# Second token mixer of a two-layer decoder trunk: shared token differences, one-instruction blends, outputs summed by channel, and a new order of the work

## The chip, the cores and the metric

The kernel runs on one core of one Trainium2 chip. That core has a matrix engine (TensorE, PE in the profile, with its weight loads as PEld), a vector engine (VectorE, DVE), a scalar engine (ScalarE, ACT), GpSimd (POOL) and a sync engine (SP) that issues the transfers. The metric is the device time of one execution in microseconds; the median of three runs before the change is 1159.81 us.

## The reference, cut to what matters

The trunk has two layers over 256 tokens of width 1024. Each is a half-step SwiGLU block, a token mixer and another half-step SwiGLU block, all between RMS norms. Layer 0 mixes with sparse attention and a state-space branch, layer 1 with RWKV-7. The change is in the second mixer, and the order of both mixers is set anew:

```python
def rwkv7_time_mix(h, mu, w_r, w_k, w_v, w_o, w0, w1, w2, a0, a1, a2, g1, g2, k_k, k_a, r_k, ln_g, ln_b):
    xx = pad(h, one token)[:, :-1] - h                    # difference to the token before
    xr, xw, xk, xv, xa, xg = [h + xx * mu[i] for i in range(6)]
    r, k, v = xr @ w_r, xk @ w_k, xv @ w_v
    w = -softplus(-(w0 + tanh(xw @ w1) @ w2)) - 0.5
    a = sigmoid(a0 + (xa @ a1) @ a2)
    g = sigmoid(xg @ g1) @ g2
    ...
    def step(state, inp):                                 # 16 heads of 64 channels, 256 steps
        sa = einsum('bhij,bhj->bhi', state, -kk_t)
        state = state * d_t + sa[..., None] * (kk_t * a_t) + v_t[..., None] * k_t
        return state, einsum('bhij,bhj->bhi', state, r_t)
    ...
    y = (y - mean) * rsqrt(var + eps)                     # by head
    y = y * ln_g + ln_b + sum(r * k * r_k) * v
    return (y * g) @ w_o
```

## The kernel before, in words

Tokens lie in two tiles (t = 0, 1) of 128, channels in eight blocks of 128. The recurrence is worked in its chunked form: each token tile is a chunk, and each chunk has two halves of eight heads, so four quarters q = 2t + half.

The stages of the second mixer (function `mix1`) are written as generators, here called strands. The parts that matter:

- `mix_k` and `mixed` blend the normed input `hT` (channels by tokens) with the token before it. `share_past` and `share_now` give the two factors mu and 1 - mu. A blend takes two instructions: `present` makes h times (1 - mu) in a small tile `mixt` on ACT or DVE, and a second one on DVE adds mu times the shifted input. There are 16 blends of 128x128 for the keys and 24 of 128x256 for r, v and the gate.
- `project_k`, `project_r`, `project_v`, `gate_in` and `gate_out` are the projections. `project_v` and `work_o` (the output projection) use three matmuls per product, with high and low parts of both operands; such three are called a triple here.
- `products` and `stored` make the triangle matrices `LT` (matmul `acc<-kk,beT`). `invert32` inverts their 32x32 diagonal blocks on DVE in 31 serial steps (tiles `lb`, `tm`, `tt`, `lc`). `invert` joins the blocks, quarter by quarter, with small matmuls (`tm,LT`, `xw,lc`, `lc,xw`, `xw,LT`, `LT,xw`) and small copies on ACT and DVE between them.
- `grams` makes three 128x128 score matrices per head, with 64 of the array's rows each (`rhT,beT`, `kk,aT`, `rhT,aT`), and `masked` multiplies them by a mask on DVE into the tiles `G` (`Gx` for quarter 2).
- `evac_v` takes the values out of PSUM: eight ACT passes over 64 columns each, with a sum, into `vc`, then on DVE the bonus product `yB` and the subtraction of the mean.
- `head` forms u for a quarter, and the carried state `Z`. `outs` forms the outputs y of a quarter: eight matmuls with the scores as weights (128 columns) and the values as the moving side (64 columns), for chunk 1 four matmuls with `rhT` as weights and Z moving, and eight more scores times u, all into one PSUM tile with tokens on the partitions. Then come the square, the norm by head, the gate, and a transpose (`tp<-ident,xu`) for the output projection.

The order is set by a planner, `_Plan`. It keeps an estimated free time for each engine and each buffer; `run` repeatedly takes the strand whose next step has the lowest sum of earliest start and priority, and every instruction is emitted on its engine in that order, which the build keeps. The priorities are the tables `PRIORITY` (second mixer) and `PRIORITY0` (first mixer). PSUM has four buffers for sums (list `pa`, tile `acc`) and two for transposes (list `pt`, tile `tp`); SBUF has `SLOTS` = 21 slots of 1024 columns.

All engine calls go through the helper `_Engine`, so that the profile gives nearly every instruction line 141; instructions are told apart by their tiles.

Of the kernel before, what the change touches and what calls it, by code (L numbers as in the profile page):

```python
# [18 lines left out]
P = 128  # L19
# [141 lines left out]
class _Strand:  # L161
    def __init__(self, gen, prio, light):
        self.gen, self.prio, self.light, self.engine, self.begin, self.end = gen, prio, light, None, 0.0, 0.0
        self.step()
# [10 lines left out]
class _Plan:  # L175
# [3 lines left out]

    AFTER = {"pe": 200.0, "act": 45.0, "dve": 45.0, "sp": 2000.0}  # L180

    def __init__(self, **free):
        self.free = {"pe": 0.0, "act": 0.0, "dve": 0.0, "sp": 0.0, **free}
        self.events, self.strands, self.now, self.users, self.load = {}, [], None, {}, []
# [35 lines left out]
    def count(self, engine, name, out, a, k):  # L220
# [5 lines left out]
        if engine == "pe":  # L226
            if name == "transpose":
# [3 lines left out]
            else:  # L231
                m = 1
                for i in a[0].shape[1:]:
                    m *= i
# [34 lines left out]
    def run(self):  # L269
        while self.strands:  # L270
            ready = [(t + s.prio + (s.light * max(0.0, self.idle(t) - 0.4) if s.light else 0.0), i) for i, s in enumerate(self.strands) if (t := self.start(s)) is not None]
# [12 lines left out]
class _Trunk:  # L284
    PRIORITY = {"factors": 100, "evac_k": 0, "products": 200, "stored": -500, "evac_r": 93, "bonus": 352, "evac_v": 417,
                "masked": -500, "second": 206, "project_k": 250, "lora": -500, "decay": 74, "rates": 73, "keys": 149,
                "invert32": 500, "mixed": -265, "split_x": -455, "project_r": 300, "gate_in": 300, "split_v": 164,
                "project_v": 406, "gate_out": 800, "grams": 43, "invert": -500, "tokens": 416, "head": 581, "outs": 869,
                "split_o": 500, "work_o": 928, "finish": 709, "ahead": 1099, "mix_k": 80}
    PRIORITY0 = {"scale": 500, "normed": 282, "work_a": 300, "end_k": 249, "end_q": -300, "end_r": -389, "split_a": 0, "split":  # L290
                 100, "project": 300, "convolved": 204, "gate": 0, "compress": -366, "attend": 141, "scores":
                 200, "values": 100, "steps": 213, "products0": 410, "tokens0": 163, "carry": 647, "decays":
                 -17, "weights": 300, "outputs": 141, "gated": 195, "project_out": 497, "summed": 324,
                 "finish": 98, "split_f": 330, "second": 200}
# [1516 lines left out]
    def mix1(self, ph, gpost, y1):  # L1811
# [3 lines left out]
        H, N, SLOTS = 16, 64, 21  # L1815
# [46 lines left out]
        pa, pt, ml, xl, gml, gl, lwl, hl, ll, rl = [0.0] * 4, [0.0] * 2, [0.0] * 3, [], [0.0], [], [0.0], [], [], [0.0] * 4  # L1862
# [3 lines left out]
        for key, n, l in (("w2", 2, lwl), ("a2", 2, lwl), ("hT", 7, xl), ("xk", 1, xl), ("rows", 1, xl), ("lc", 4, sl),  # L1866
                          ("lws", 2, xl), ("XW0", 2, xl), ("XW1", 2, xl), ("rowb", 2, sl), ("rowg", 4, sl),
                          ("gtk", 2, sl), ("btk", 2, sl), ("tm", 4, hl), ("Z", 4, lwl)):
            share(key, n, l)
# [20 lines left out]
        xk = self.xp.tile([P, KD, S], F32, name="mix", tag="x8")  # L1890

# [53 lines left out]
        def mix_k(t):  # L1945

            for k in range(KD):
                e = plan.sooner("act", "dve")
                yield e, ml
                m = mt([P], "mixt")  # L1950
                present(e, m, 2, k, P * t, P * t + P)
                yield "dve"
                nc.vector.scalar_tensor_tensor(xk[:, k, TS[t]], *self.share_past(2, k, P * t, P * t + P), m, op0=ALU.mult, op1=ALU.add)
                give(ml)
                fire("xk", t, k)
            drop("hT")

        def second():
# [27 lines left out]
            add(mix_k(1), pr["mix_k"])  # L1986
# [271 lines left out]
        def mixed(name, i, buffers):  # L2258

            for k in range(KD):  # L2260
                e = plan.sooner("act", "dve")
                yield e, ml, ev("h"), *([buffers] if k == 0 else [])
                if k == 0:
                    X[name] = (self.xp if name == "r" else mp).tile([P, KD, S], F32, name="mix", tag="x8" if name == "r" else "mix")
                m = mt([S], "mixt")
                present(e, m, i, k, 0, S)
                yield "dve"
                nc.vector.scalar_tensor_tensor(X[name][:, k], *self.share_past(i, k, 0, S), m, op0=ALU.mult, op1=ALU.add)
                give(ml)
            drop("hT")  # L2270
# [91 lines left out]
        def evac_v(t, c, a):  # L2362
# [3 lines left out]
            yield "act", *([] if vc[t] else [sl])  # L2366
# [7 lines left out]
            nc.vector.tensor_scalar(mean, mean, -1.0 / N, None, op0=ALU.mult)  # L2374
# [3 lines left out]
            yield "dve"  # L2378
# [463 lines left out]
```

## Time and profile before

| | |
|---|---|
| median of the runs | 1159.81 us (1159.47 to 1159.92) |
| profiled execution | 1158.96 us, of which span 1157.2 us |
| PE busy | 1137.4 us, 98% |
| DVE busy | 941.3 us, 81% |
| ACT busy | 679.8 us, 59% |
| granted PE clock | 0.998 |
| second mixer | about 741 to 967 us of the span |

A row of the view by order of time has start, length, engine, line, operation, and tiles as out<-in; for a matmul the moving operand stands first and the weights second, then rows*columns of the array that it uses, then the size of the result, and the number of rows that were put together. An f32 matmul leaves two such rows, one in the rounded format (the triples and the bulk of the SwiGLU blocks) one. In the view of windows, a window's start and end are followed by its length and by the busy time and count of each engine. In the view of groups, a busy sum and the mean of one in ns are followed by the engine's idle time before the group and what ended it.

### The profile page before, as it was taken

Reading aid. Unit: us, or ns where it says so; the run is one execution under the profiler, and the core shown is the slowest. Engines: PE = TensorE matmul, PEld = TensorE weight load, DVE = VectorE, ACT = ScalarE, POOL = GpSimd, SP = SyncE. Lnnn points to the kernel's source line nnn. Section 1 sums busy time; section 2 is a strip of 40 time slices with the busy share of each in tenths; the row PEclk is TensorE's granted clock in tenths of the full one; section 3 lists DMA queues with packets and bytes.
Section 4 is the critical chain, followed back from the end, with each engine's and each line's share of the span. In section 5 each row is a group of like instructions: output and inputs, shape, how many; then the busy total and the mean of one; then the engine's idle time right before and its main releaser. Section 6 shows DMA issues by size and latency. Waiting matters only on the chain.

```text
span 1157.2 us, 17665 instructions
## 1 busy us (share of the span) xinstructions
PE 1137.4 (98%) x6771; PEld 959.0 (83%) x6771; DVE 941.3 (81%) x1495; ACT 679.8 (59%) x1105; POOL 17.2 (1%) x46
## 2 busy tenths in 40 slices
PE   9999999999999999999999999999999999999997
PEld 7788888888988778888888888799988797888885
DVE  6696697898779889977889969678885798899694
ACT  6655465677574786655687755475054135877461
POOL 0000000000000000000000000002100000000000
PEclk9999999999999999999999999999999999999999
DMA  8857535433334735735462845611333022718631
GB/s 281 288 190 242 193 128 186 149 129 109 110 125 161 268 121 204 251 146 197 160 262 95 296 173 217 229 38 50 120 111 146 20 109 92 309 55 278 228 118 68
DMA packets 50131, 192.42 MB, mean 166 GB/s; under 512 B 6205, under 2 KB 6205, under 8 KB 46334
## 3 DMA queue, kind: packets, MB, share of 16 engines
q1 hardware_dynamic: 50046, 191.29, 46.4%
q8 instruction: 53, 0.87, 0.3%
q14 instruction: 32, 0.26, 0.1%
HBM read 190.22 MB, written 1.05 MB: 165 GB/s over the span
## 4 chain that ended last, share of the span: by engine, by line
PE 76%; DVE 9%; DMA 6%; ACT 5%; issue 3%; SPq 0%; DVEq 0%; ACTq 0%
PE acc L141 72%; PE tp L141 4%; DVE wlo L141 3%; DMA raw<-in_wst_dram 3%; ACT whi L141 2%; DMA hx<-in_wst_dram 2%; DMA wa<-in_wst_dram 1%; ACT junk L141 1%; DVE hx L141 1%; DVE rs_a L141 1%; ACT hx L141 1%; ACT wa L141 0%; DVE suml L141 0%; DVE rs_y L141 0%; DVE x L141 0%
## 5 line engine op out<-in xcount | busy, mean ns | idle before, releaser
L141 ACT ACTIVATE whi<-raw,gch 128x1024 fp32r<-128x1024 f32 (+2 forms) x187 | 186.1, 1016 | 95.8 <-DMA raw<-in_wst_dram 76.3
L141 DVE SCALAR_TENSOR_TENSOR wlo<-raw,gch,whi 128x1024 fp32r<-128x1024 f32 (+2 forms) x187 | 204.4, 1113 | 38.7 <-ACT whi L141 38.1
L141 PE MATMUL acc<-wlo,xth 128*128 128x512 f32 (+1 forms) x536 | 207.4, 390 | 0.8 <-DVE wlo L141 0.8
L141 PE MATMUL acc<-whi,xtl 128*128 128x512 f32 (+1 forms) x536 | 206.8, 389 | 0.0
L141 PE MATMUL acc<-whi,xth 128*128 128x512 f32 (+1 forms) x536 | 203.7, 392 | 0.7 <-ACT whi L141 0.5
L141 PEld LDWEIGHTS acc<-whi,xth 128*128 128x128 f32 x536 | 100.6, 188 | 21.8 <-ACT whi L141 1.5
L141 PEld LDWEIGHTS acc<-wlo,xth 128*128 128x128 f32 x536 | 100.6, 188 | 21.3 <-DVE wlo L141 1.8
L141 PEld LDWEIGHTS acc<-whi,xtl 128*128 128x128 f32 x536 | 100.5, 188 | 20.1 <-DVE xtl L141 0.4
L141 DVE TENSOR_TENSOR wlo<-raw,whi 128x1024 fp32r<-128x1024 f32 x80 | 97.0, 1223 | 16.2 <-ACT whi L141 15.5
L141 PE MATMUL acc<-whi,hx 128*128 128x512 f32 x320 | 102.2, 390 | 0.0
L141 ACT CAST whi<-raw 128x1024 fp32r<-128x1024 f32 x80 | 83.3, 1051 | 30.4 <-DMA raw<-in_wst_dram 15.5
L141 PE MATMUL acc<-whi,xt 128*128 128x512 f32 x312 | 97.7, 391 | 0.0
L141 PEld LDWEIGHTS acc<-whi,hx 128*128 128x128 f32 x320 | 60.1, 188 | 12.4
L141 PEld LDWEIGHTS acc<-whi,xt 128*128 128x128 f32 x312 | 58.4, 188 | 11.9
L141 PE MATMUL acc<-wlo,hx 128*128 128x512 f32 x160 | 61.9, 389 | 0.0
L141 PE MATMUL acc<-wlo,xt 128*128 128x512 f32 x156 | 60.9, 393 | 0.4 <-DVE wlo L141 0.3
L141 DVE TENSOR_TENSOR wlo<-wa,whi 128x1024 fp32r<-128x1024 f32 x42 | 50.8, 1220 | 9.9 <-ACT whi L141 9.8
L141 ACT CAST whi<-dr 128x1024 fp32r<-128x1024 f32 x32 | 33.4, 1053 | 29.4 <-DVE dr L141 16.8
L141 ACT ACTIVATE sg<-acc,rs_y 128x512 f32<-128x512 f32 (+1 forms) x45 | 29.0, 644 | 36.7 <-PE acc L141 36.7
L141 ACT CAST whi<-wa 128x1024 fp32r<-128x1024 f32 x42 | 43.5, 1050 | 11.5 <-DMA wa<-in_wst_dram 5.5
L141 PE MATMUL acc<-xnh,whi 128*128 128x256 f32 x160 | 46.6, 291 | 0.0
L141 PE MATMUL acc<-xnl,whi 128*128 128x256 f32 x160 | 45.2, 282 | 0.0
(408 smaller groups left out, 2397.7 us busy)
## 6 DMA issues: line engine op xcount, KB each, us to landing
raw<-in_wst_dram SPq DMA_DIRECT2D x244, 512.0 KB, 4.3
wa<-in_wst_dram SPq DMA_DIRECT2D x14, 1024.0 KB, 7.3
dr<-in_wst_dram SPq DMA_DIRECT2D x8, 1024.0 KB, 6.0
hx<-in_wst_dram SPq DMA_DIRECT2D x6, 1024.0 KB, 8.0
lw<-in_wst_dram SPq DMA_DIRECT2D x12, 512.0 KB, 3.5
whi<-in_wst_dram SPq DMA_DIRECT2D x8, 512.0 KB, 5.9
wlo<-in_wst_dram SPq DMA_DIRECT2D x8, 512.0 KB, 6.1
wr<-in_wst_dram SPq DMA_DIRECT2D x8, 512.0 KB, 6.4
```

Of the source, the lines that this page charges most:

```text
L141: r = f(out, *a, **k)
```

## The change

Five edits in the second mixer, one in the planner, and two new tables.

1. `turned(t)` forms xx, the difference of a token to the one before it, once for each token tile, in four instructions of 128x512 on DVE. `blend` then makes each blend from xx, mu and hT in one DVE instruction; `present` and the tiles `mixt` are gone.
2. `evac_v` takes the sum by head with one DVE reduction over 128x512, scales it, and adds it to the values on the way out of PSUM; the eight ACT passes are gone, and the bonus product comes after.
3. `outs` swaps the sides: the values (64 columns) are the weights and the scores (128 columns) move, so that a result has a head's 64 channels on the partitions, even heads in the lower and odd heads in the upper half. The four matmuls on Z swap sides too. The sum is copied to SBUF by ACT or DVE, whichever the planner has free sooner, and turned back by four transposes into a second PSUM buffer (`acc<-ident,xu`); from there on all is as before.
4. `tokens` puts its two results in one tile of 2048 columns, which takes over the place of xx; `SLOTS` goes from 21 to 19.
5. In `outs` the eight score matmuls are one step for the planner; before, it could put other work after every second one.
6. The planner notes the array shape of a strand's matmuls (`mode`) and could add `SWITCH` for a change of shape; `SWITCH` is 0.0.
7. All entries of `PRIORITY` but one and eight of the 28 of `PRIORITY0` have new values, and with them the order of both mixers changes.

```diff
-    PRIORITY = {"factors": 100, "evac_k": 0, "products": 200, "stored": -500, "evac_r": 93, "bonus": 352, "evac_v": 417,
+    PRIORITY = {"factors": 136, "evac_k": -73, "products": 254, "stored": -554, "evac_r": 62, "bonus": 241, "evac_v": 388,
...
-        def present(e, m, i, k, t0, t1):
-            h, mu = self.share_now(i, k, t0, t1)
-            if e == "act":
-                nc.scalar.activation(m, h, AF.Copy, scale=mu)
-            else:
-                nc.vector.tensor_scalar(m, h, mu, None, op0=ALU.mult)
+        def turned(t):
+            ts = slice(P * t, P * t + P)
+            for h in range(2):
+                yield "dve", *([ev("h")] if t else [])
+                ks = slice(4 * h, 4 * h + 4)
+                nc.vector.tensor_sub(xx[:, ks, ts], self.hT[:, ks, P * t:P * t + P], self.hT[:, ks, 1 + P * t:1 + P * t + P])
+                fire("xx", t, h)
+            drop("hT")
+
+        def blend(out, i, k, t0, t1):
+            nc.vector.scalar_tensor_tensor(out, xx[:, k, t0:t1], self.mu[:, 0, 8 * i + k:8 * i + k + 1], self.hT[:, k, 1 + t0:1 + t1],
+                                           op0=ALU.mult, op1=ALU.add)
...
-                e = plan.sooner("act", "dve")
-                yield e, ml
-                m = mt([P], "mixt")
-                present(e, m, 2, k, P * t, P * t + P)
-                yield "dve"
-                nc.vector.scalar_tensor_tensor(xk[:, k, TS[t]], *self.share_past(2, k, P * t, P * t + P), m, op0=ALU.mult, op1=ALU.add)
-                give(ml)
+                yield "dve", ev("xx", t, k // 4)
+                blend(xk[:, k, TS[t]], 2, k, P * t, P * t + P)
                 fire("xk", t, k)
...
-            for j in range(8):
-                if j:
-                    yield "act"
-                hs = slice(N * (8 * c + j), N * (8 * c + j) + N)
-                nc.scalar.activation(vc[t][:, hs], a[:, N * j:N * j + N], AF.Identity, accum_out=mean[:, j:j + 1])
+            nc.vector.tensor_reduce(mean, hd(a), axis=mybir.AxisListType.X, op=ALU.add)
+            nc.vector.tensor_scalar(mean, mean, -1.0 / N, None, op0=ALU.mult)
+            nc.vector.tensor_add(hd(vc[t][:, cs]), hd(a), bcH(mean, 8))
+            fire("v", t, c)
...
-            yp = acc()
+            yt = acc((4, P))
+            at = lambda j: yt[N * (j % 2):N * (j % 2) + N, j // 2, :]
             for j in range(8):
-                nc.tensor.matmul(yp[:, N * j:N * j + N], G[j][:, 2, :], vh(j), start=j == 0, stop=False)
-                if j % 2 == 1:
-                    yield "pe"
+                nc.tensor.matmul(at(j), vh(j), G[j][:, 2, :], start=j < 2, stop=False)
             if c == 1:
+                yield "pe"
                 for m in range(4):
-                    nc.tensor.matmul(yp[:, P * m:P * m + P], rhT[c][:, 4 * half + m, :], f2(Z[0][:, 4 * half + m]), start=False, stop=False)
-                yield "pe"
+                    nc.tensor.matmul(yt[:, m, :], f2(Z[0][:, 4 * half + m]), rhT[c][:, 4 * half + m, :], start=False, stop=False)
                 drop(("rh", c), "Z")
+            yield "pe"
             for j in range(8):
-                nc.tensor.matmul(yp[:, N * j:N * j + N], G[j][:, 0, :], u[:, N * j:N * j + N], start=False, stop=j == 7)
-                if j % 2 == 1 and j < 7:
-                    yield "pe"
+                nc.tensor.matmul(at(j), u[:, N * j:N * j + N], G[j][:, 0, :], start=False, stop=j > 5)
...
+            e = plan.sooner("act", "dve")
+            yield e
+            (nc.scalar.copy if e == "act" else nc.vector.tensor_copy)(XU[q][:, 0], f2(yt))
+            give(pa)
+            yield "pe", pa
+            yp = acc()
+            for m in range(4):
+                nc.tensor.transpose(yp[:, P * m:P * m + P], XU[q][:, 0, P * m:P * m + P], self.ident)
```

Three places of the order show what moved. The first is PE at the outputs of the last two quarters (`Z,rhT` and `rhT,Z` are the state's part; `wh,oT` and `wl,oT` the output projection). Before:

```order
L141 MATMUL acc<-vc,Gx 128x64 x8
L141 MATMUL acc<-Z,rhT 128x128 x4
L141 MATMUL tp<-ident,xu 128x128 x4
L141 MATMUL acc<-xu,Gx 128x64 x8
L141 MATMUL acc<-vc,G 128x64 x8
L141 MATMUL acc<-Z,rhT 128x128 x4
L141 MATMUL acc<-xu,G 128x64 x8
L141 MATMUL acc<-wh,oT 128x512
```

Now, from quarter 2's outputs to the turn back of quarter 2:

```order
L141 MATMUL acc<-Gx,vc 64x128 x8
L141 MATMUL acc<-rhT,Z 128x128 x4
L141 MATMUL acc<-Gx,xu 64x128 x8
L141 MATMUL acc<-wh,oT 128x512
L141 MATMUL acc<-wl,oT 128x512
L141 MATMUL acc<-wh,oT 128x512 x2
L141 MATMUL acc<-wl,oT 128x512
L141 MATMUL acc<-wh,oT 128x512
L141 MATMUL tp<-ident,xu 128x128 x4
L141 MATMUL acc<-ident,xu 128x128 x4
```

The results are 64 partitions by 128 columns where they were 128 by 64, the output projection starts between two quarters' outputs, and the turn back (`acc<-ident,xu`) stands behind six of its matmuls.

The second place is PE at the inverse (`whi,mix` and `wlo,mix` are the value projection's triples). Before:

```order
L141 MATMUL acc<-lc,xw 32x32 x16
L141 MATMUL acc<-whi,mix_7393 128x512
L141 MATMUL acc<-wlo,mix_7393 128x512
L141 MATMUL acc<-whi,mix_7590 128x512
L141 MATMUL acc<-xw,LT 64x64 x8
L141 MATMUL acc<-whi,mix_7393 128x512
L141 MATMUL acc<-wlo,mix_7393 128x512
L141 MATMUL acc<-whi,mix_7590 128x512
L141 MATMUL acc<-xw,LT 64x64 x8
L141 MATMUL acc<-LT,xw 64x64 x8
```

Now, from the last triple on:

```order
L141 MATMUL acc<-whi,mix_7461 128x512
L141 MATMUL tp<-ident,aT 128x128 x4
L141 MATMUL acc<-tm,LT 32x32 x48
L141 MATMUL tp<-ident,aT 128x128 x4
L141 MATMUL acc<-xw,lc 32x32 x8
L141 MATMUL acc<-lc,xw 32x32 x16
L141 MATMUL tp<-ident,beT 128x128 x4
L141 MATMUL acc<-xw,lc 32x32 x8
L141 MATMUL acc<-lc,xw 32x32 x16
L141 MATMUL acc<-rhT,beT 128x128 x2
L141 MATMUL acc<-kk,aT 128x128 x2
L141 MATMUL acc<-rhT,aT 128x128 x2
```

No triple stands between the steps of the inverse any more, nor between the groups of scores behind it: all 36 matmuls that stood there come ahead of it, and transposes and scores stand in their place.

The third place is DVE in the last steps of `invert32`. Before, two splits of value weights (`wlo`) stood among all its steps, the second of them here:

```order
L141 TENSOR_TENSOR wlo<-lw,whi 128x1024
L141 TENSOR_TENSOR tm<-lb,tt 128x27x5
L141 TENSOR_TENSOR tt<-tt,tm 128x27x5
L141 TENSOR_TENSOR tm<-lb,tt 128x28x4
L141 TENSOR_TENSOR tt<-tt,tm 128x28x4
L141 TENSOR_TENSOR tm<-lb,tt 128x29x3
L141 TENSOR_TENSOR tt<-tt,tm 128x29x3
L141 TENSOR_TENSOR tm<-lb,tt 128x30x2
```

Now:

```order
L141 TENSOR_TENSOR vc<-acc,vm 128x512
L141 TENSOR_TENSOR yB<-acc,bon 128x512
L141 TENSOR_TENSOR tm<-lb,tt 128x28x4
L141 TENSOR_TENSOR tt<-tt,tm 128x28x4
L141 TENSOR_REDUCE vm<-acc 128x8
L141 TENSOR_SCALAR vm<-vm 128x8
L141 TENSOR_TENSOR vc<-acc,vm 128x512
L141 TENSOR_TENSOR wlo<-lw,whi 128x1024
L141 TENSOR_TENSOR yB<-acc,bon 128x512
L141 TENSOR_TENSOR wlo<-lw,whi 128x1024
L141 TENSOR_TENSOR tm<-lb,tt 128x29x3
L141 TENSOR_TENSOR tt<-tt,tm 128x29x3
```

Five weight splits and two evacuations of values now stand among the steps of `invert32`.

More of the change, by code (lines that the diff above doesn't have):

```diff
@@ L162, in __init__ @@
     def __init__(self, gen, prio, light):
-        self.gen, self.prio, self.light, self.engine, self.begin, self.end = gen, prio, light, None, 0.0, 0.0
+        self.gen, self.prio, self.light, self.engine, self.begin, self.end, self.mode = gen, prio, light, None, 0.0, 0.0, None
         self.step()
@@ L183, in __init__ @@
         self.free = {"pe": 0.0, "act": 0.0, "dve": 0.0, "sp": 0.0, **free}
-        self.events, self.strands, self.now, self.users, self.load = {}, [], None, {}, []
+        self.events, self.strands, self.now, self.users, self.load, self.mode = {}, [], None, {}, [], (0, 0)
     def event(self, *key):
@@ L226, in count @@
         if engine == "pe":
+            m = 1
+            for i in a[0].shape[1:]:
+                m *= i
+            mode = (a[0].shape[0] <= 64) + (a[0].shape[0] <= 32), (m <= 64) + (m <= 32)
+            self.mode = self.now.mode = mode
             if name == "transpose":
@@ L270, in run @@
         while self.strands:
-            ready = [(t + s.prio + (s.light * max(0.0, self.idle(t) - 0.4) if s.light else 0.0), i) for i, s in enumerate(self.strands) if (t := self.start(s)) is not None]
+            ready = [(t + s.prio + (s.light * max(0.0, self.idle(t) - 0.4) if s.light else 0.0) + self.SWITCH * (s.want[0] == "pe" and s.mode not in (None, self.mode)), i) for i, s in enumerate(self.strands) if (t := self.start(s)) is not None]
             assert ready, [(s.gen.__name__, s.want) for s in self.strands]
@@ L1985, in second @@
             fire("h")
-            add(mix_k(1), pr["mix_k"])
+            add(chain(turned(1), mix_k(1)), pr["mix_k"])
         def lora(t):
@@ L2260, in mixed @@
             for k in range(KD):
[L2261 to L2262 removed]
+                yield "dve", ev("xx", 1, k // 4), *([buffers] if k == 0 else [])
                 if k == 0:
                     X[name] = (self.xp if name == "r" else mp).tile([P, KD, S], F32, name="mix", tag="x8" if name == "r" else "mix")
[L2265 to L2270, printed above, removed]
+                blend(X[name][:, k], i, k, 0, S)
+            drop("hT", "xx")
             fire("x", name)
@@ L2487, in tokens @@
         def tokens():
-            for name, src, n in (("gtk", gaT, "ga"), ("btk", beT, "be")):
-                yield "act", ev("ga", 0), ev("L", 1), sl
-                d = by[name] = slot([D], name)
+            yield "act", ev("ga", 0), ev("L", 1), dl
+            two = double([2, D], "by")
+            for i, (name, src, n) in enumerate((("gtk", gaT, "ga"), ("btk", beT, "be"))):
+                d = by[name] = two[:, i]
                 for h in range(2):
@@ L2683, in mix1 @@
         add(second(), pr["second"])
-        add(mix_k(0), pr["mix_k"])
+        add(chain(turned(0), mix_k(0)), pr["mix_k"])
         add(chain(project_k(0), project_k(1)), pr["project_k"])
```

41 lines of the change are left out of this document (18 added, 23 removed).

## The prediction

> **What bounds the kernel now.** I read the page's busy lines and its chain first, then the stretch of the second mixer (741 to 967 us) by windows, by waits and by order of time.
>
> ```profile
> span 1157.2 us, 17665 instructions
> PE 1137.4 (98%) x6771; PEld 959.0 (83%) x6771; DVE 941.3 (81%) x1495; ACT 679.8 (59%) x1105; POOL 17.2 (1%) x46
> PE 76%; DVE 9%; DMA 6%; ACT 5%; issue 3%; SPq 0%; DVEq 0%; ACTq 0%
> ```
>
> TensorE (PE) is busy 98% of the span, and the chain runs through it for 76%. A microsecond taken out of its stream is worth a microsecond, unless another engine then comes last. Two of five windows of the mixer, and the sum of the five (the one before the first head begins with the inverse):
>
> ```profile
> 816.00:854.80 38.80, 38.14 (x272) 35.20 (x271) 36.13 (x80) 9.31 (x41) 5.23 (x15) 1.00 0.31 113
> 854.80:897.30 42.50, 42.07 (x656) 35.19 (x656) 25.90 (x61) 19.58 (x72) 1.11 (x1) 1.00 0.38 138
> sum 225.90, PE 222.03 PEld 198.43 DVE 174.59 ACT 96.64 POOL 14.73; mean PE 44.41 PEld 39.69 DVE 34.92 ACT 19.33 POOL 2.95
> ```
>
> The columns are window, length, then busy time of PE, weight load, DVE, ACT and POOL, then the granted clock, which is 1.00. Over 225.9 us PE lacks 3.9 us, DVE has 174.6 us (77%), ACT 96.6 us. DVE is the only engine near enough to take over; in 816 to 854.8 it is busy 36.1 of 38.8 us, with the 31 serial steps of the inverse. What PE waited for from 741 to 975 us:
>
> ```profile
> PE tp L141 <- DVE xn L141: 1.7, 1, 1.7
> PE tp L141 <- ACT sq L141: 1.3, 1, 1.3
> PE acc L141 <- DVE tm L141: 0.7, 1, 0.7
> PE acc L141 <- ACT xw L141: 0.3, 1, 0.3
> ```
>
> The first lies ahead of the mixer's first matmul and stays.
>
> **The change part by part.** First the outputs. Each f32 matmul stands in the trace as two rows, so eight heads are 16 rows:
>
> ```profile
> 935.53 0.60 PE L141 MATMUL tp<-ident,xu 128*128 128x128 f32 x4
> 935.97 1.90 PE L141 MATMUL acc<-xu,Gx 128*128 128x64 f32 x16
> 937.70 1.95 PE L141 MATMUL acc<-vc,G 128*128 128x64 f32 x16
> 939.49 1.11 PE L141 MATMUL acc<-Z,rhT 128*128 128x128 f32 x8
> ```
>
> From start to start, 16 rows of the old form (128 weight columns, 64 moving) take 939.49 - 937.70 = 1.79 us, 112 ns each. The new form (64 weight columns, 128 moving, heads alternating between the two column halves) already stands in the first mixer:
>
> ```profile
> 347.44 0.39 PE L141 MATMUL acc<-seg,stT 128*64 128x128 f32 x4
> ...
> 350.50 0.39 PE L141 MATMUL acc<-seg,stT 128*64 128x128 f32 x4
> 350.82 0.50 PE L141 MATMUL acc<-whi,yt 128*128 128x512 f32 x1
> ```
>
> Between the two quoted pieces lie 14 steps of 4 rows: 3.06 us for 56 rows, 55 ns each. The four output strands hold 4 x 32 = 128 rows: 128 x (112 - 55) = 7.3 us saved. The four matmuls per strand on the carried state (Z) only swap sides; both are 128 wide, so they cost the same. The turn back adds 16 transposes; four took 935.97 - 935.53 = 0.44 us, in all 1.76 us. Net -5.5 us.
>
> A change of tile shape costs PE time too. The end of a scores group and the projection triple after it:
>
> ```profile
> 882.64 0.39 PE L141 MATMUL acc<-kk,aT 64*128 64x128 f32 x4
> 882.86 0.39 PE L141 MATMUL acc<-rhT,aT 64*128 64x128 f32 x4
> 883.18 0.50 PE L141 MATMUL acc<-whi,mix 128*128 128x512 f32 x1
> 883.52 0.39 PE L141 MATMUL acc<-wlo,mix 128*128 128x512 f32 x1
> 883.75 0.40 PE L141 MATMUL acc<-whi,mix 128*128 128x512 f32 x1
> ```
>
> Four rows go in 0.22 us and a triple's matmul in 0.23 us, but 882.86 to 883.18 and 883.18 to 883.52 take 0.10 and 0.11 us more: 0.2 us per change of shape. I counted the changes along the two PE orders of the second mixer: 51 before, 47 now. The outputs add about a dozen, and taking twelve triples out of the inverse and the scores removes more. 4 x 0.2 = 0.8 us saved. In the first mixer the count is 35 in both, with the same instructions, and PE has hardly any wait there; I put its new order at 0 and keep -1 to +1.5 us.
>
> Next what DVE and ACT get. Rows that price it:
>
> ```profile
> L141 DVE TENSOR_TENSOR G<-acc,tb 128x384 f32<-128x384 f32 x24 | 11.9, 552 | 11.0 <-PE acc L141 11.0
> L141 DVE TENSOR_TENSOR wlo<-lw,whi 128x1024 fp32r<-128x1024 f32 x8 | 9.8, 1221 | 0.3 <-ACT whi L141 0.2
> L141 DVE TENSOR_SCALAR mixt<-hT,mu 128x128 f32<-128x128 f32 x11 | 3.1, 280 | 0.0
> L141 DVE TENSOR_TENSOR yB<-acc,bon 128x512 f32<-128x512 f32 x4 | 2.7, 687 | 0.0
> L141 DVE TENSOR_REDUCE gn<-xu 128x8 f32<-128x512 f32 x4 | 2.7, 680 | 0.0
> L141 ACT ACTIVATE mixt<-hT,mu 128x256 f32<-128x256 f32 x23 | 11.4, 505 | 1.3 <-DVE mix L141 1.3
> L141 ACT ACTIVATE vc<-acc 128x64 f32<-128x64 f32 x32 | 6.8, 227 | 3.7 <-PE acc L141 3.6
> L141 ACT COPY xu<-acc 128x512 f32<-128x512 f32 x4 | 2.3, 587 | 22.2 <-PE acc L141 22.2
> ```
>
> Blends: the 40 products with the present share go (ACT at least 11.4 us, DVE at least 3.1 us); four subtractions of 128x512 come, at about 0.69 us each (nearest row: yB) 2.8 us of DVE. The 40 blends stay. Means: ACT loses 32 small passes (6.8 us and their accumulator reads); DVE gets four reductions at 0.68 us, 2.7 us. Outputs: four copies of 128x512, 0.59 us on ACT or 0.69 on DVE. So ACT drops by 18 us or more, DVE rises by 2.4 us (-3.1 + 2.8 + 2.7) to 5.2 us. None of it is on PE's path by itself: cover is 225.9 - 174.6 = 51 us of DVE idle time in the mixer. At the mixer's start the blend waits for two subtractions (1.4 us), but 32 rows on the projection of the decay and rate stand first on PE, and afterwards each blend needs one instruction instead of two on two engines. I take 0; without that cover it would cost 1.4 us. Lighter ACT should bring the squares (sq) in time: -1.3 us at most, 0 at least; I take -1.0 us, because in the new order 26 and 42 projection matmuls stand before the last two of those steps.
>
> Now the moved work. Twelve triples (36 matmuls, 36 x 0.23 = 8.2 us) that stood inside the inverse and the scores now stand before the inverse. Two places decide whether PE then waits.
>
> First, the start of the inverse:
>
> ```profile
> 813.12 1.71 PE L141 MATMUL acc<-kk,beT 64*128 64x128 f32 x16
> 819.31 2.00 DVE L141 STREAM_TRANSPOSE lb<-lc 128x1024 f32<-128x1024 f32 x1
> 852.70 1.98 DVE L141 STREAM_TRANSPOSE tm<-tt 128x1024 f32<-128x1024 f32 x1
> 854.83 1.88 PE L141 MATMUL acc<-tm,LT 64*32 64x32 f32 x64 [0.69 <-DVE tm L141]
> ```
>
> and, from the groups by line:
>
> ```profile
> L141 DVE COPY lc<-LT 32x256 f32<-32x256 f32 x8 | 5.1, 641 | 0.3
> L141 DVE TENSOR_TENSOR rhT<-acc,E 128x256 f32<-128x256 f32 x8 | 3.0, 419 | 0.7 <-PE acc L141 0.6
> ```
>
> PE needs 854.83 - 814.8 - 0.69 = 39.3 us from the last triangle product; with 8.2 us more and two projection steps less, 47.0 us. DVE's part from lb to the end of tm is 35.4 us; to it come three more weight splits (3 x 1.22) and two evacuations of the values (2 x (0.68 + 0.17 + 0.69 + 0.69), the 0.17 a small operation), 8.1 us, so 43.5 us. It starts about 2.8 us after the last product (ahead stand one scaling of 0.69, two lc copies of 0.64, two rhT products of 0.42) rather than 4.5. That is 46.3 against 47.0: the wait of 0.7 us goes, but only just. I take -0.5 us, bounds -0.7 and +2.
>
> Second, the scores. In the new order eight groups of six matmuls follow each other with nothing between. A group takes PE 12 x 0.056 = 0.67 us, and DVE two masks of 0.55 us, 1.1 us. Eight groups: 8.8 us of DVE, 5.4 of PE; four accumulators let PE run two groups (1.1 us) ahead, so PE waits 8.8 - 5.4 - 1.1 = 2.3 us. Queued behind the last masks on DVE are one row addition (1.22 us) and the scaling of u, for which the state update waits; about 6 us of PE work stands between, so it is covered. Bounds: 0 if the masks keep up with the groups spread through the inverse, +4 if DVE enters the row late.
>
> Sum: -5.5 - 0.8 - 1.0 - 0.5 + 2.3 = -5.5 us; 0.2 us for a first wait at some turn (transposes wait for the copy of 0.6 us; at least two gate matmuls or six projection matmuls stand between) makes -5.3 us. The profiled execution took 1158.96 us (span 1157.2 and 1.76 around it), so it becomes 1153.7; the median of the runs is 0.85 above it, hence 1154.5 us.
>
> [...] The recorded weight loads:
>
> ```profile
> L141 PEld LDWEIGHTS tp<-vc,gtk x32: 133/136/138, 905.0 to 906.7; 128*64 128x64 f32 x32
> L141 PEld LDWEIGHTS acc<-vc,G x96: 186/192/192, 890.9 to 939.3; 128*128 128x128 f32 x96
> ```
>
> 64 columns more cost 192 - 136 = 56 ns of loading. If the load of a half-width weight could not run under the other half's matmul, a row would take 55 + 56 = 111 ns, and the swap would save nothing: -5.3 + 7.2 gives 1161.7 us. [...]
>
> **The rivals.** (B) The cover is thin: the mask wait is at its +4, the inverse starts 2 us late instead of earlier. 1154.5 + (4 - 2.3) + (2 + 0.5) = 1158.7, no change to be told. For it: 46.3 against 47.0 us. Against: DVE is idle 16.6 of the 42.5 us from 854.8.
>
> (C) Slower, by one mechanism: the inverse runs bare. Each quarter has three hand-offs (small products to ACT copies, to the 64-wide products, to ACT copies); the triples between them were their cover. The only one uncovered before cost 0.3 us (xw above). If all 12 are exposed by one ACT copy of 0.59 us and those 0.3 us again, 12 x 0.89 = 10.7 us are lost: 1165.2 us. It decides from 0.64 us per hand-off on (12 x 0.64 = 7.6, the 5.3 us saved and the 2.3 us that can be told). Against it: transposes, scores and the other quarters' products still stand between the stages.
>
> [...] (E) Every stall goes: no mask wait, -1.3 and -0.7 in full: 1154.5 - 2.3 - 0.5 - 0.2 = 1151.5.
>
> **How the numbers follow.** Forecast 0.66, with its own range 1152.3 to 1157; E 0.05; B 0.16; C 0.10; D 0.03. A run of this kernel tells 0.2%, 2.3 us, from no change: below 1157.5 is faster, above 1162.1 slower. Faster: 0.66 + 0.05 and a quarter of B, 0.75. Same: the rest of B and D, 0.15. Slower: C, 0.10. The range for 8 in 10 reaches from 1151.5 (E) to 1159.5 (most of B) and leaves out C, D and a little at either end.
>
> **What would show it.** Right: the output rows 55 ns apart in the form 128*64 128x128; 16 new transposes at 0.11 us; PE's busy time in the mixer lower by about 6 us with waits of 2 to 5 us; the mask group still ended by PE, with PE waiting on G in the row of eight. Wrong: output rows 110 ns apart (D); PE waits on ACT xw or LT that sum to several microseconds (C); a wait for tm over 2 us (B); a longer stretch from 190 to 380 us, which would be the first mixer's order and no part of my sum.

## The result: 11.7 us faster, where 5.3 us were forecast

The median went from 1159.64 us (1159.28 to 1159.92, four runs) to 1147.95 us (1147.24 to 1149.64, four runs), a ratio of 0.9901 with a 95% interval of 0.9884 to 0.9919. The time lies 3.55 us below the range of the prediction. The direction was right, the size was more than double.

Three rows of the page of the kernel after:

```profile
span 1145.8 us, 17597 instructions
PE 1128.3 (98%) x6787; PEld 953.8 (83%) x6787; DVE 940.0 (82%) x1486; ACT 664.9 (58%) x1022; POOL 17.0 (1%) x46
PE 83%; DVE 7%; DMA 5%; ACT 3%; issue 2%; SPq 0%; DVEq 0%; ACTq 0%
```

The span fell by 11.4 us. To see where, I cut it at two landmarks that all these kernels have: PE's first matmul on the decay weights (`hT,lws`) and the first matmul of the last SwiGLU block (`whi,xt`). Between them lies the second mixer. The view of windows for exactly that stretch (window, length, busy time of PE, weight load, DVE, ACT and POOL, clock), first before:

```profile
743.50:967.10 223.60, 220.77 (x2060) 197.59 (x2061) 173.17 (x376) 96.01 (x250) 13.30 (x27) 1.00 0.25 92
```

and after:

```profile
743.40:956.30 212.90, 212.80 (x2076) 192.03 (x2077) 172.44 (x370) 80.82 (x164) 13.12 (x27) 1.00 0.28 97
```

The mixer takes 10.7 us less. What lies ahead of it is 0.2 us shorter, what lies behind it 0.6 us; both are within the scatter, for in the traces of the experiments below the part ahead takes 741.6 to 743.9 us (the kernel with a price on changes of shape left aside) and the part behind 189.4 to 190.9 us. PE's idle time in the mixer fell from 2.83 to 0.10 us: nothing waits any more that this view can see. ACT lost 15.2 us, DVE 0.7 us. The view of PE's waits from 741 to 965 us, after, has two lines left, both outside the stretch:

```profile
PE tp L141 <- DVE xn L141: 1.7, 1, 1.7
PE tp L141 <- DVE x L141: 0.6, 1, 0.6
```

One quarter's outputs after, by order of time:

```profile
911.94 1.45 PE L141 MATMUL acc<-lw,sgT 128*128 128x512 f32 x3
913.32 1.09 PE L141 MATMUL acc<-G,vc 128*64 128x128 f32 x16
914.34 0.66 PE L141 MATMUL tp<-ident,xu 128*128 128x128 f32 x4
914.93 1.09 PE L141 MATMUL acc<-G,xu 128*64 128x128 f32 x16
915.95 1.55 PE L141 MATMUL acc<-lw,sgT 128*128 128x512 f32 x3
```

Sixteen rows of the new form take 914.34 - 913.32 = 1.02 us: 16 x 55 ns are 0.88 us, and the changes of shape on either side account for the rest: by the starts, the first and the last of the eight matmuls take 0.16 and 0.21 us instead of 0.11.

I then went through PE's rows in both traces and set the time from each start to the next against the usual spacing of its form. With the run below that puts the outputs back, this splits the 11.4 us by the terms of the prediction. Its -0.8 us for the changes of shape is taken apart into eleven that the outputs bring and fifteen that the order takes away, 0.2 us each (the counts are those of the orders: 51 before, 36 with the new order and old outputs, 47 after). The second row of the table is what the other rows leave of the total.

| term | forecast, us | measured, us |
|---|---|---|
| output rows, turn back and eleven changes of shape | -5.5 + 2.2 = -3.3 | -4.03 |
| fifteen changes of shape fewer, and all rows named nowhere else | -3.0 | -3.42 |
| single waits (squares, inverse, its copies, values, turned outputs; 3.4 to 0.2) | -1.3 | -3.2 |
| waits on the masks (1.94 to 1.93) | +2.3 | 0.0 |
| ahead of the mixer and behind it | 0 | -0.75 |
| sum | -5.3 | -11.4 |

### The profile page after: what moved, and what is told of

The parts are those of the page before. It is cut to its first block, busy times and chain, and to the rows that moved or that the text cites. A ratio compares the mean times of both kernels' runs of the same rounds, so it can differ in the third digit from the quotient of the medians.

```text
span 1145.8 us, 17597 instructions
## 1 busy us (share of the span) xinstructions
PE 1128.3 (98%) x6787; PEld 953.8 (83%) x6787; DVE 940.0 (82%) x1486; ACT 664.9 (58%) x1022; POOL 17.0 (1%) x46
## 4 chain that ended last, share of the span: by engine, by line
PE 83%; DVE 7%; DMA 5%; ACT 3%; issue 2%; SPq 0%; DVEq 0%; ACTq 0%
PE acc L141 78%; PE tp L141 5%; DVE wlo L141 3%; DMA raw<-in_wst_dram 3%; ACT whi L141 2%; DMA wa<-in_wst_dram 1%; DMA hx<-in_wst_dram 1%; ACT junk L141 0%; DVE u L141 0%; DMA dr<-in_wst_dram 0%; DVE x L141 0%; DVE rs_a L141 0%; DVE hx L141 0%; DVE dr L141 0%; SPq L320 0%
## 5 line engine op out<-in xcount | busy, mean ns | idle before, releaser
L141 DVE TENSOR_TENSOR wlo<-raw,whi 128x1024 fp32r<-128x1024 f32 x80 | 96.7, 1221 | 16.6 <-ACT whi L141 16.1
```

The source lines that it names most:

```text
L141: r = f(out, *a, **k)
```

## The experiments

Single executions of one kernel differ by 1 to 3 us either way, and more where the granted clock fell in one of them, which the last section takes up. So beside each median stands the length of the second mixer in the profiled execution (223.6 us before, 212.9 or, unrounded, 212.96 us after), which shows which part moved. The kernel with the first mixer's old order has the changed kernel's second mixer, matmul for matmul, and took 213.25 us there: 0.3 us is what two traces of one mixer differ by. Unless a text says otherwise the granted clock was 1.00 throughout.

**The outputs put back.** The changed kernel with the old `outs`:

```diff
-                nc.tensor.matmul(at(j), vh(j), G[j][:, 2, :], start=j < 2, stop=False)
+                nc.tensor.matmul(yp[:, N * j:N * j + N], G[j][:, 2, :], vh(j), start=j == 0, stop=False)
```

> The changed kernel with the outputs in their old form (weights 128 columns wide, 64 moving, no turn back); order tables, blends and value evacuation stay new. Mine, from the two traces: 128 rows go back from 55 to 112 ns, +7.3 us; 16 transposes go, -1.8 us; and the second mixer has 36 instead of 47 changes of tile shape, 11 x 0.2 = -2.2 us: about +3.3 us against the changed kernel (1151.2). Rival: the changes of shape at the outputs are covered and cost nothing: +5.5 us (1153.4). Second rival: the outputs are where all of the unforeseen gain lies (the old form waited elsewhere too): +9 us or more.

Median 1152.73 us (1150.68 to 1153.81, five runs), second mixer 217.0 us: the outputs are worth 4.03 us there, between my 3.3 and the rival's 5.5. So the changes of shape do take part of the gain back. Some 0.5 us of the 4.03 is neither rows nor changes: the 48 rows of scores of the last quarter take 3.83 us with the old outputs and 3.38 us in the changed kernel. The rows next to a change (one ahead, two behind) carry 5.9 us beyond their usual spacing here, with 36 changes, and 8.1 us in the changed kernel with 47: 0.16 and 0.17 us a change, against 9.5 us for 51 before.

**The second mixer's order put back.**

```diff
-    PRIORITY = {"factors": 136, "evac_k": -73, "products": 254, ...
+    PRIORITY = {"factors": 100, "evac_k": 0, "products": 200, ...
```

> The changed kernel with the second mixer's old order table; outputs, blends and evacuation stay new. Changes of tile shape 57 instead of 47. Theory order: the stalls that went (squares 1.3, inverse 0.7, xw 0.3, values 0.3, turned outputs 0.4 us, in all 3 us) went by the order, and the shapes add 10 x 0.2 = 2 us: +5 us (1152.9). Theory lighter ACT: those stalls stay away with less work on ACT, only the shapes come back: +2 us (1150).

Median 1154.01 us (1153.30 to 1154.93), second mixer 220.0 us, 7.1 us longer than with the new order and more than either theory said. The longest waits of PE inside the mixer:

```profile
PE tp L141 <- DVE xu L141: 1.4, 2, 0.9
PE acc L141 <- DVE tm L141: 1.0, 1, 1.0
PE tp L141 <- ACT sq L141: 0.7, 1, 0.7
PE acc L141 <- ACT xu L141: 0.7, 1, 0.7
```

The squares and the inverse are waited for as before the change, though ACT is as light as in the changed kernel. The wait of 0.7 us on ACT's `xu` is new: there the old order has nothing on PE between the outputs and the turn back, which needs ACT's copy. The two on DVE's `xu` are transposes for the output projection that wait for a quarter just turned back; the kernel before has one such wait, of 0.3 us.

**The first mixer's order put back.**

```diff
-    PRIORITY0 = {"scale": 573, "normed": 282, ...
+    PRIORITY0 = {"scale": 500, "normed": 282, ...
```

> The changed kernel with the first mixer's old order table and all else new. Mine: the trace of the first mixer is 0.2 us shorter after the change, so +0.2 us, not to be told from none. Rival: the first mixer's order gives 1 to 1.5 us that the single profile hides.

Median 1150.30 us (1147.02 to 1153.58, six runs), 2.35 us above the changed kernel. The profiled execution is the fastest of the six; its span is 1145.3 us, and what lies ahead of the second mixer takes 742.2 us against 743.4 with the new order. The trace shows no gain by the first mixer's new order, while the median does, and the times of the two kernels overlap. The rival's 1 to 1.5 us stay open.

**The order alone.** The kernel before with the new `PRIORITY` and nothing else.

> The kernel before with the second mixer's new order table alone; outputs, blends, evacuation and the first mixer's table stay old. Changes of tile shape 43 instead of 51, -1.6 us. Theory order: the stalls of 3 us go too: -4 to -5 us against the kernel before (1155). Theory lighter ACT: the stalls stay or grow since ACT still has the blends' products: -1.6 us to +1 us (1158 to 1160.6).

Median 1158.14 us (1155.53 to 1163.71, twelve runs; four of these had a clock of 0.991, the median of the other eight is 1157.14), ratio 0.9997 (0.9982 to 1.0013). Second mixer 221.5 us: -2.1 us, nearer to the second theory, where the same table is worth 7.1 us with the rest of the change. PE is idle 3.4 us of it. The longest wait, with ACT's rows at that place:

```profile
860.93 0.33 ACT L141 ACTIVATE vc<-acc 128x64 f32<-128x64 f32 x1
861.03 0.32 ACT L141 ACTIVATION_READ_ACCUMULATOR vc<-acc 128x1 f32 x1
861.12 1.19 ACT L141 COPY gtk<-tp 128x512 f32<-128x512 f32 x2
```

```profile
859.12 1.03 PE L141 MATMUL tp<-ident,aT 128*128 128x128 f32 x8
861.88 0.66 PE L141 MATMUL tp<-ident,beT 128*128 128x128 f32 x4 [1.72 <-ACT gtk L141]
```

The last of 16 small evacuation passes, which began at 857.96, stand in ACT's queue ahead of the copy `gtk`. PE's next transposes need the buffer that this copy empties. ACT is idle 125 of the 221.5 us, and yet PE waits for it.

**ACT's load put back, PE's order held.** An operation that the planner's books do not see leaves the order as it is. So one can give ACT its old work again and have PE (and here DVE) execute the changed kernel's order, instruction for instruction.

```diff
         def blend(out, i, k, t0, t1):
+            keep, plan.now = plan.now, None
+            nc.scalar.activation(mt([t1 - t0], "mixt"), self.hT[:, k, 1 + t0:1 + t1], AF.Copy, scale=self.mu[:, 1, 8 * i + k:8 * i + k + 1])
+            plan.now = keep
```

> The changed kernel, PE's and DVE's order unchanged to the instruction; ahead of each of the 40 blends ACT gets back the product of a token with its share (16 of 128x128, 24 of 128x256, about 17 us of ACT), whose result nobody reads. Theory lighter ACT: the stalls that the new order had alone (1.9 us on the turned tokens, 0.9 us on the inverse, 1.3 us around the masks) come from ACT's load and return: the second mixer gets 2 to 4 us longer (1150 to 1152). Theory order: ACT has room also with this load (81 + 17 of 213 us), what counts is the order that is planned for the content: less than 0.5 us.

Median 1150.26 us (1149.89 to 1152.05), second mixer 215.0 us: +2.0 us, the least that the first theory said, but not at the places that it named. There is one wait more, on the squares. ACT and PE there:

```profile
775.79 2.45 ACT L141 ACTIVATE mixt<-hT,mu 128x128 f32<-128x128 f32 x8
...
779.08 0.65 ACT L141 ACTIVATE sq<-kk 128x512 f32<-128x512 f32 x1
```

```profile
779.77 1.10 PE L141 MATMUL tp<-hsel,sq 128*128 128x64 f32 x8 [1.56 <-ACT sq L141]
```

Eight products of the keys' second half (2.45 us) stand ahead of `sw`, `ks` and `sq`.

The same with the values' evacuation, whose sum goes back to eight ACT passes:

```diff
-            nc.vector.tensor_reduce(mean, hd(a), axis=mybir.AxisListType.X, op=ALU.add)
+            plan.spend("dve", 150 + 1.05 * 8)
+            keep, plan.now = plan.now, None
+            for j in range(8):
+                nc.scalar.activation(vc[t][:, 512 * c + N * j:512 * c + N * j + N], a[:, N * j:N * j + N], AF.Identity, accum_out=mean[:, j:j + 1])
+            plan.now = keep
```

> The changed kernel, PE's order unchanged to the instruction; the evacuation of the values is done by the old instructions (eight small passes with a sum on ACT instead of one reduction on DVE), which stand in ACT's queue where the planner had the reduction. Theory queue: in the kernel with the new order alone the wait of 1.7 us for the turned tokens comes from 16 such passes (3.2 us) ahead of their copy on ACT; here a pack of 8 (1.7 us) stands ahead of the inverse's copies, and PE waits 1 to 2 us more. Theory planned order: those waits come from the order that the table gives for other content, not from the passes: less than 0.5 us, or shorter (DVE gets 2.7 us less).

Median 1150.93 us (1148.69 to 1160.99, ten runs), 3.0 us above the changed kernel. Its profiled execution is the one of 1160.99 us, in which the clock fell, so its stage length says nothing. Beside the waits of the changed kernel it has 1.0 us on `sg` (a gate in ACT's queue, behind a pack of passes) and 0.7 us on `LT`, at the inverse. Both loads together:

> The changed kernel, PE's order unchanged to the instruction, with both ACT loads back: the 40 products ahead of the blends (nobody reads them) and the evacuation by eight small passes. If ACT's load is what separated the order alone (second mixer 221.5 us) from order with lighter ACT (217.0 us with the old outputs), 3.5 to 4.5 us come back here: the second mixer takes 216.5 to 217.5 us. If it is the order planned for the content: 2 us from the wait for the squares, as with the products alone, and no more: 215 us.

Median 1152.25 us (1149.91 to 1163.59, ten runs), second mixer 217.5 us. The lines of PE's waits inside the mixer that the changed kernel has not, and the window of the mixer:

```profile
PE tp L141 <- ACT sq L141: 1.6, 1, 1.6
PE tp L141 <- ACT sg L141: 1.0, 1, 1.0
PE acc L141 <- ACT LT L141: 1.0, 2, 0.7
```

```profile
741.60:959.10 217.50, 213.83 (x2076) 192.26 (x2077) 170.09 (x366) 101.70 (x268) 13.13 (x27) 1.00 0.27 95
```

The wait on `LT` begins on DVE, which stands still for ACT's passes and then comes late to all its copies for the inverse:

```profile
863.56 0.17 DVE L141 TENSOR_SCALAR vm<-vm 128x8 f32<-128x8 f32 x1 [3.01 <-ACT vc L141]
```

ACT's old load costs 217.53 - 212.96 = 4.57 us with PE's order unchanged. From the other side, order alone against order with lighter ACT (the run with the old outputs) is 221.54 - 216.99 = 4.55 us. So in this order the lighter ACT is worth about 4.6 us. That the two agree so closely is chance, for the waits are not the same ones: `sq`, `sg` and `LT` here, in all 3.6 us (where the other 1.0 us lies was not traced), and `gtk`, `G` and `LT` in the order alone. It acts by the place in the queue: ACT is busy 102 of 217 us here.

**Lighter ACT alone.** The kernel before with the differences, the one-instruction blends and the evacuation on DVE; old tables, old outputs.

> The kernel before with the blends by differences and the values' evacuation on DVE, but the old order tables and the old outputs. From the sum of what is measured (old order with lighter ACT and new outputs -3.6 us, new outputs alone -2.3 us, both in the second mixer): -1.3 us if the parts add up, second mixer 222.3 us. Theory lighter ACT by itself: the waits for the squares, the inverse and the values (2.3 us) go: -2.3 us. Theory of my prediction: -1.0 us (squares).

Median 1157.67 us (1154.20 to 1160.45, ten runs), ratio 0.9979 (0.9966 to 0.9991), second mixer 221.8 us: -1.8 us, between the two theories. This kernel also has the one tile of 2048 columns and the 19 slots (edit 4), which no run tests alone. Of the waits of before, three are left:

```profile
PE acc L141 <- DVE tm L141: 1.0, 1, 1.0
PE tp L141 <- ACT sq L141: 0.7, 1, 0.7
PE acc L141 <- DVE vc L141: 0.3, 1, 0.3
```

**The new outputs alone,** in the kernel before:

> The kernel before with the outputs in the new form alone (64-wide weights, turned back by transposes); old order tables, blends, evacuation. Row arithmetic: -7.3 + 1.8 us, and 56 instead of 51 changes of shape at 0.1 to 0.2 us each, +0.5 to +1.0: -4.5 to -5 us (1155). Rival: in the old order nothing covers the copy between the outputs and their transposes (0.6 us and the hand-over, four strands), 2 to 3 us are given back: -2 us (1157.5).

Median 1157.75 us (1155.90 to 1161.13, ten runs), ratio 0.9989 (0.9976 to 1.0002), second mixer 221.3 us: -2.3 us. The rival holds. The places, in PE's order of time:

```profile
934.20 0.66 PE L141 MATMUL tp<-ident,xu 128*128 128x128 f32 x4 [0.69 <-DVE xu L141]
...
937.46 0.66 PE L141 MATMUL acc<-ident,xu 128*128 128x128 f32 x4 [0.69 <-ACT xu L141]
...
939.49 0.73 PE L141 MATMUL acc<-wh,oT 128*128 128x512 f32 x2 [0.92 <-DVE oT L141]
```

The three parts one by one in the second mixer: order -2.1, lighter ACT -1.8, outputs -2.3, together -6.2 us. The change has -10.7. The missing 4.5 us belong to no part alone. The lists of waits point to the reason: each part alone ends in waits that are gone when the others are there.

**Narrower masks.** PE's order held again; this tests whether DVE paces the rows of scores.

```diff
-            nc.vector.tensor_mul(Gs[q][j], ps[:, 1:4, :], gmask[:, 1:4, :])
+            plan.spend("dve", 150 + 1.05 * 384)
+            keep, plan.now = plan.now, None
+            nc.vector.tensor_mul(Gs[q][j][:, 0:2], ps[:, 1:3, :], gmask[:, 1:3, :])
+            nc.scalar.activation(Gs[q][j][:, 2], gmask[:, 1], AF.Copy, scale=0.0)
+            plan.now = keep
```

> The changed kernel, PE's order unchanged to the instruction; each of the 32 masks multiplies two of the three products of a head (256 columns instead of 384), and ACT writes zeros in place of the third, so the outputs lack the part that goes straight from the values. Theory: in the rows of scores PE runs at DVE's pace, 2 x 0.474 us a group against 0.67 us of its own; with narrower masks (about 0.34 us) the 1.5 us that PE waits in the row of eight and 0.4 us in the last quarter go: second mixer 1.5 to 1.9 us shorter. Rival: 0.93 us per group is PE's own pace in this form (hand-over of accumulators), nothing changes: 0 to -0.3 us.

Second mixer 211.55 us, 1.4 us less; median 1146.53 us (1145.94 to 1147.66). The row of eight is 1.3 us shorter; in the last quarter, where 0.4 us was expected, only 0.06 us goes. The starts of groups in the row of eight, in the changed kernel (PE, then DVE over the same time):

```profile
885.98 0.62 PE L141 MATMUL acc<-rhT,beT 64*128 64x128 f32 x2
...
886.91 0.62 PE L141 MATMUL acc<-rhT,beT 64*128 64x128 f32 x2
```

```profile
883.29 4.74 DVE L141 TENSOR_TENSOR G<-acc,tb 128x384 f32<-128x384 f32 x10 [1.76 <-PE acc L141]
887.95 3.80 DVE L141 TENSOR_TENSOR Gx<-acc,tb 128x384 f32<-128x384 f32 x8
```

and with the narrow masks:

```profile
884.48 0.39 PE L141 MATMUL acc<-rhT,beT 64*128 64x128 f32 x4
...
885.15 0.39 PE L141 MATMUL acc<-rhT,beT 64*128 64x128 f32 x4
```

```profile
883.34 3.44 DVE L141 TENSOR_TENSOR G<-acc,tb 128x256 f32<-128x256 f32 x10 [2.03 <-PE acc L141]
```

A group went every 0.93 us, as DVE's masks do in a row (4.74 us for ten, two to a group), and goes every 0.67 us, PE's own time, when a mask takes 0.34 us. So PE waited for the masks in the row of eight. The kernel before has the same step in its short rows of groups; one position in two groups that follow each other there, and DVE's masks over that time:

```profile
922.23 0.27 PE L141 MATMUL acc<-rhT,beT 64*128 64x128 f32 x1
...
923.16 0.27 PE L141 MATMUL acc<-rhT,beT 64*128 64x128 f32 x1
```

```profile
920.94 3.81 DVE L141 TENSOR_TENSOR G<-acc,tb 128x384 f32<-128x384 f32 x8 [1.43 <-PE acc L141]
```

Again 0.93 us, and DVE's masks stand in a row at 0.476 us each. The view of waits has no line for it, in the changed kernel as in the one before: an f32 row's modelled length runs over the gap to the next. In the changed kernel's row of eight the starts 885.98 and 886.23 us are 0.25 us apart, and the row at 885.98 is recorded at 0.27 us.

**Outputs in one piece.** The state's four matmuls first, then both runs of half-wide weights without a step between:

```diff
+            if c == 1:
+                for m in range(4):
+                    nc.tensor.matmul(yt[:, m, :], f2(Z[0][:, 4 * half + m]), rhT[c][:, 4 * half + m, :], start=m == 0, stop=False)
...
-            yield "pe"
             for j in range(8):
                 nc.tensor.matmul(at(j), u[:, N * j:N * j + N], G[j][:, 0, :], start=False, stop=j > 5)
```

> The changed kernel with each output strand in one piece, the state's four matmuls first, so that the two runs of half-wide weights of a quarter stand together: 42 instead of 47 changes of tile shape. Theory: a change of shape at the outputs costs 0.1 to 0.2 us of PE: -0.5 to -1.0 us (1147). Rival: the pieces in one lose their place between transposes and copies, and a wait eats it: 0 to +1 us.

Median 1148.04 us (1146.29 to 1150.03), second mixer 213.1 us: no change. The rows next to a change of shape carry 7.1 instead of 8.1 us, as the theory said (5 x 0.2), and the rival's wait takes most of it back:

```profile
PE tp L141 <- DVE xu L141: 0.7, 1, 0.7
```

**A price on changes of shape in the planner.**

```diff
-    SWITCH = 0.0
+    SWITCH = 400.0
```

> The changed kernel with a price of 400 ns on a change of tile shape in the planner's choice (0 before): 44 instead of 47 changes, and another order in many places. If a change of shape is what an order is worth: 3 x 0.15 to 0.3 us, -0.5 to -0.9 us in the second mixer. If stalls decide (an order that was not fitted to the waits): +1 to +4 us, as the other tables that were not fitted to their content.

Median 1175.50 us (1173.69 to 1176.35), ratio 1.0131 (1.0116 to 1.0146), far beyond both expectations. The price also reorders the first mixer: what lies ahead of the second takes 753.9 us, 10.5 us more, with two waits on `wlo`, 7.1 us in all, and about 10 us at half clock around them. The second mixer takes 230.5 us, 17.6 more, in which PE waits 3.0 us on `x` and 4.4 us on `xu` and runs at half clock for 13.7 us, from between these two waits on. Three changes of shape fewer are worth nothing beside that.

No version here beats the changed kernel by more than the times scatter; narrow masks, which leave work out, come nearest, with a median 1.4 us lower.

## Why the prediction was right or wrong, point by point

**Output rows, -5.5 us: right.** With the changes of shape that come with it the new form is worth 4.03 us, where rows and changes together gave 3.3; some 0.5 us of it is a shorter row of scores and no part of my sum. The rival by the weight loads (D, 1161.7 us) is out: it needs 111 ns a row, 1.8 us for 16, and they take 1.02 us. The 111 ns were my estimate from the recorded loads, 55 + 56, and no run shows them: both column halves use all 128 rows, and 16 rows whose loads are recorded at 137 ns each, 2.19 us in all, go in 1.02 us.

**Changes of shape, -0.8 us: right within what the runs resolve.** A change costs 0.16 to 0.19 us over all of them (5.9 us for 36, 9.5 for 51). Rows next to a change went from 9.5 to 8.1 us, -1.4. The kernel with the outputs in one piece has five changes fewer and 1.0 us less beside them.

**Single waits, -1.3 us: mis-sized.** I took 1.0 of the 1.3 us on the squares, 0.5 of 0.7 on the inverse, nothing for three smaller lines, and added 0.2 us for a wait at some turn. All of them went but 0.2 us, and no new one came: -3.2 us. It took both order and load: with lighter ACT and the old order the squares and the inverse are still waited for (0.7 and 1.0 us); with the new order alone they are not, but others come, and PE is idle 3.4 us in all. The start of the inverse came as worked out: its last transpose on DVE ends at about 859.2 us, PE's first matmul on it starts at 859.69, a margin of 0.5 us where 0.7 was forecast.

**Masks, +2.3 us: wrong.** This is the step that failed most: "Eight groups: 8.8 us of DVE, 5.4 of PE; four accumulators let PE run two groups (1.1 us) ahead, so PE waits 8.8 - 5.4 - 1.1 = 2.3 us." The mechanism exists, as the narrow masks show. A mask in a row costs 0.474 us, not the 0.55 us of a single one; with that the same sum gives 16 x 0.474 - 5.4 - 1.1 = 1.1 us, and narrow masks took 1.3 us out of that row. What failed is the step from this wait to a change: the kernel before had such waits too, in its own short rows of groups, 1.94 us by the spacing of the starts, and I took the view of waits, which has no line for them, as proof that there were none. After the change it is 1.93 us, so what changed was 0.0 us. The 1.94 us, and the 0.5 us after the change that narrow masks left, rest on the spacing alone; no run with narrow masks was made of the kernel before.

**ACT's 18 us, put at 0: the load was about right, the reason for 0 wrong.** ACT lost 15.2 us net, with all four new copies in it. DVE, forecast to gain 2.4 to 5.2 us, lost 0.7: it got no copy, and its 40 blends, as long as before (480 ns for 256 columns in both, 349 and now 343 ns for 128), now run back to back (14.3 us busy instead of 16.6). "None of it is on PE's path by itself: cover is 225.9 - 174.6 = 51 us of DVE idle time" looked at DVE, which gets work, and not at ACT, which loses it. ACT's work was on PE's path in packs: 16 evacuation passes ahead of a copy, eight products ahead of a square. With that load back and PE's order held, 4.6 us return. The wait on the squares among them (1.6 us) is one that the kernel before had too; those on `sg` and `LT` (2.0 us) are in neither trace of before and after: they come with the new order when ACT has its old load, as the 0.7 us on `LT` in the order alone.

**The rivals.** B (1158.7) and C (1165.2) needed waits at the inverse; there is none in the changed kernel. C's picture of bare hand-offs comes true only with the small passes on ACT (0.7 us on `LT` once), and then far from 10.7 us. E (every stall goes, 1151.5) named the right mechanism at 0.05, but it took away only the waits that the sum listed, not the small lines and not what changed outside the mixer, and left the outputs 0.7 us too small; the result lies 3.55 us below it.

**The first mixer's order, 0: not settled.** The two main traces differ by 0.2 us ahead of the second mixer; with the old table put back the trace is 1.2 us shorter there and the median 2.35 us longer.

**The interaction: not in the prediction at all.** I added the edits up as if each were worth the same with or without the others. Their parts alone make 6.2 us; that this is near the 5.3 us forecast is chance, for 5.3 has 2.3 us of mask waits taken off that did not come. Together they make 10.7 in the mixer.

## What to carry to other kernels

When PE is 98% busy, an edit is worth what the next queue allows: price edits that share an order together, and ask of each helper engine not how busy it is but what stands in its queue ahead of the one copy that PE needs. Before a new wait is charged, look whether the old kernel pays it already: take the spacing of starts in the trace, since the list of waits can miss one that modelled ends cover. To separate load from order, add or remove an operation without letting the planner see it, so that the bounding engine's order stays the same.

## What the runs showed of the hardware that was not expected

The granted clock fell to a half for a stretch in some executions. In the kernel with the price on changes of shape, after a wait of 3.0 us (windows as above):

```profile
958.00:963.00 5.00, 1.56 (x11) 0.87 (x9) 4.55 (x16) 3.08 (x7) 0.00 (x0) 0.96 0.76 311
963.00:968.00 5.00, 0.91 (x4) 0.72 (x4) 4.73 (x13) 0.28 (x1) 0.00 (x0) 0.50 0.00 0
968.00:973.00 5.00, 3.79 (x9) 2.43 (x9) 4.62 (x15) 0.59 (x1) 0.00 (x0) 0.50 0.00 0
976.00:979.00 3.00, 3.00 (x14) 2.46 (x13) 0.17 (x1) 0.00 (x0) 0.00 (x0) 0.96 0.00 0
```

PE is busy 2.5 of the first 10 us and runs at 0.50 until about 976 us. The rows of PE that end its two long waits there:

```profile
961.28 1.38 PE L141 MATMUL tp<-ident,x 128*128 128x128 f32 x8 [3.01 <-DVE x L141]
967.09 1.09 PE L141 MATMUL tp<-ident,xu 128*128 128x128 f32 x4 [4.43 <-DVE xu L141]
```

The mean of 0.96 over the first window puts the fall 0.4 us before its end, at about 962.6 us: after the wait of 3.0 us and eight transposes, ahead of the wait of 4.4 us. The same trace has a clock of 0.59 from 754 to 756 us, right after a wait of only 1.65 us, which the kernel before and the changed one have too (1.66 us in both) and pass at 1.00.

In the second case there is no long wait: PE waits 1.0 us on `sg` and 0.7 us on `LT` from 840 to 905 us. In the profiled execution with the evacuation on ACT:

```profile
868.00:870.00 2.00, 1.26 (x23) 1.07 (x20) 1.89 (x6) 1.45 (x4) 0.00 (x0) 1.00 0.00 0
870.00:872.00 2.00, 2.00 (x50) 1.76 (x48) 1.57 (x5) 1.31 (x3) 0.00 (x0) 0.93 0.04 8
874.00:896.00 22.00, 22.00 (x231) 20.39 (x231) 7.00 (x14) 7.60 (x28) 0.00 (x0) 0.50 0.08 25
898.00:900.00 2.00, 2.00 (x31) 2.00 (x30) 1.74 (x4) 0.00 (x0) 0.00 (x0) 0.75 0.00 0
```

PE ran at half clock for 27 us, from about 871.7 to 899 us, though by the trace it was busy all that time; this execution took 10 us more than the others of the same kernel. A wait of 0.7 us among small matmuls stands 2.6 us ahead of the fall. That it is the cause is not shown, for the trace with both loads has the same wait at the same place and stays at 1.00. The row with the evacuation on ACT, then with both loads:

```profile
869.13 1.14 PE L141 MATMUL acc<-xw,LT 64*64 64x64 f32 x16 [0.74 <-ACT LT L141]
```

```profile
869.54 0.68 PE L141 MATMUL acc<-xw,LT 64*64 64x64 f32 x8 [0.73 <-ACT LT L141]
```

A fall, told by a mean clock of 0.985 to 0.991, came in one of ten executions of this kernel, one of ten with both loads, four of twelve with the order alone and all four with the price on changes of shape. The first three are kernels in which PE waits among the small matmuls of the inverse or of the score groups; but so does the kernel before (0.3 us on `xw`). None of the executions of the kernel before and of the change that were timed here shows a clock below 0.996. Why these and not others stays open; no run tested it.
